# First stage of a decoder trunk: raw input blocks transposed as they land, the norm's factors applied to the weights and to the results

## The chip, the core and the metric

The kernel runs on one core of a Trainium2 chip. The core has five engines, each with an instruction queue of its own: TensorE (PE; its weight loads are listed as PEld), VectorE (DVE), ScalarE (ACT), GpSimd (POOL) and SyncE (SP, which here issues most of the transfers). PE reads from the on-chip buffer and writes its sums into eight accumulator banks (PSUM); ACT and DVE read those banks, POOL does not in this kernel. The engines wait for each other and for transfers by semaphores. The metric is the device time of one execution in microseconds (us).

## What is computed

The reference is a trunk of two layers over 512 positions of 1024 channels. The part that matters here is the beginning of the first layer: a norm of the input, and a projection of it to queries, keys and values of three head groups.

```python
def rms_norm(x, g):
    x32 = x.astype(jnp.float32)
    y = x32 * lax.rsqrt(jnp.mean(x32 * x32, axis=-1, keepdims=True) + EPS)
    return (y * g.astype(jnp.float32)).astype(x.dtype)

def dilated_mixer(xn, w_qkv, w_o, cos, sin):
    qkv = xn @ w_qkv                       # (512, 1024) @ (1024, 2304)
    q, k, v = jnp.split(qkv, 3, axis=-1)
    q = apply_rope(q.reshape(B, T, A_HEADS, HEAD_DIM), cos, sin)
    k = apply_rope(k.reshape(B, T, A_HEADS, HEAD_DIM), cos, sin)
    ...                                    # three groups: banded attention with dilation 1, 4, 16
    return o.reshape(B, T, A_WIDTH) @ w_o

# in reference(), layer 0:
    mix = dilated_mixer(rms_norm(h, g[0]), w_qkv_a[l], w_o_a[l], cos, sin)
```

Behind it follow the attention, a gated feed-forward layer with a short convolution, a shared key/value projection, a second attention and a second feed-forward layer. None of that is changed.

The norm of a row is the row times one number (the reciprocal root of its mean square) times one weight per channel. So `rms_norm(x, g) @ W` equals `diag(r) @ (x @ (diag(g) @ W))`, with `r` one number per position.

## The kernel before

**Precision.** All products are made from halves. A number is split into a high part, rounded to the product's format by a copy, and a low part, the difference; `mm3` (L263) then issues three products: high by high, high by low, low by high (L264, L265, L266). Activations are split when they leave the accumulators, weights by the class `Weights`.

**Weights.** `Weights` (L35) holds a list of pieces of 512 KB, in the order of their use: four pieces for queries and keys of group 0 (pieces 0 to 3, two 128-row chunks each), two for values of group 0 (4 and 5, four chunks each), four for queries and keys of group 1 (6 to 9), four of group 2 (10 to 13), four for values of groups 1 and 2 (14 to 17), then the output projection and the rest of the trunk. `load` issues a piece's transfers on SP (L49), `high` makes the high half on ACT (L57), `low` the low half on DVE (L69). `split(n)` does this up to piece n, `get` hands out the next piece and keeps `ahead` pieces split in advance. Each call of `high` also issues the loads of two pieces more.

**Order.** There is no planner: every engine runs its instructions in the order of the program's text. So the order of the calls at the first stage's end (L1252 to L1289) is the order of work on each engine. SP's transfers are in one queue; the built program gives them eight counters in turn, and a transfer waits until the eighth one before it has landed.

**First stage.** The 512 positions are four blocks of 128. x arrives block by block (`load_x`), interleaved with the weight pieces. The norm's weights arrive as one row, are split in halves on DVE (L246, L247) and spread over all 128 partitions by four products with a row of ones into two PSUM banks (`gain0`, L252). Around these stand warm-up products on zeros (`warm_up`, L231). Then, for each block b:

- the mean square on ACT, the root on ACT, the reciprocal on DVE (`rstd_h`, L268; for block 0 `rstd_shared`, L280, in which ACT and DVE take half of the columns each);
- the norm on DVE, twice 512 columns, times the reciprocal root and times `gain0` (`normed`, L298);
- eight transposes of 128 by 128 on PE into two banks, high halves on ACT (L355), low halves on DVE (L356): `transpose_in` (L342) fills `xT`;
- `qk0`: for each of eight chunks of channels three products of 512 columns into the block's bank, queries and keys of group 0 side by side;
- `qk_post`: ACT copies the bank (L1071), POOL applies the rotary tables (L1077 to L1080).

POOL's `reorder` (L1060) then copies `xT` into `xP`, with positions sorted by their remainder by 4, which groups 1 and 2 use. After the last block, `v_proj0` makes the values of group 0 (L1209; products of 256 columns, `v_ps`), `wide_proj` queries and keys of groups 1 and 2 (`qk_ps` from `xP`) and the values of both, and in between stand the transposes of queries and keys, the scores, the softmax and the probabilities' transposes. DVE also adds rows of the feed-forward weights (`down_sums`) in this time; their transfers go through SP too.

Small tiles come from pools in rotation: `t4` tiles (ten of 4 KB per partition) hold raw weight pieces, x after the norm, rows, values; `t8` tiles (sixteen of 8 KB) hold split pieces and `xT`, `xP`; `bank` hands out the eight PSUM banks in turn.

Of the kernel before, what the change touches and what calls it, by code (L numbers as in the profile page):

```python
# [34 lines left out]
class Weights:  # L35
# [3 lines left out]
    def __init__(self, nc, new_raw, new_pair, pieces):  # L39
        self.nc, self.new_raw, self.new_pair, self.pieces = nc, new_raw, new_pair, pieces  # L40
        self.ahead, self.ahead_dma = 4, 2
        self.raw, self.ready, self.half_done = {}, {}, []
        self.n_dma = self.n_split = self.n_get = 0
# [9 lines left out]
    def high(self, minus=False):  # L53
        if self.n_split < len(self.pieces):
            self.load(self.n_split + 1 + self.ahead_dma)
            raw, pair = self.raw.pop(self.n_split), self.new_pair()
            self.nc.scalar.copy(pair[:, 0], raw)  # L57
            self.half_done.append((raw, pair))
            if minus:
                self.minus()  # L60
# [5 lines left out]
    def low(self):  # L66
        if self.half_done:
            raw, pair = self.half_done.pop()
            self.nc.vector.tensor_tensor(pair[:, 1], raw, pair[:, 0].bitcast(F32), ALU.subtract)  # L69
            self.ready[self.n_split] = (pair[:, 0], pair[:, 1])  # L70
            self.n_split += 1
# [32 lines left out]
def trunk_kernel(ctx, tc, x, norm_gains, w_qkv_a, w_o_a, w_q_b, w_o_b, kv_norm, w_kvf, b_f,  # L104
# [14 lines left out]
    def t4(shape, dt=F32, name="t4"):  # L119
        return p4.tile(shape, dt, tag="t4", name=name)  # L120
# [99 lines left out]
    g_row = t4([1, D], name="g_row")  # L220
    sp.dma_start(g_row, norm_gains[0:1, 0, :])
    ones = sml.tile([1, 128], F32R, tag="ones", name="ones", bufs=1)
    dve.memset(ones.bitcast(F32), 1.0)
# [8 lines left out]
    load_x(0)  # L232
    W.load(3)
    load_x(1)
    W.load(4)
    load_x(2)
# [8 lines left out]
    gr = t4([1, D], F32R, name="gain_h"), t4([1, D], F32R, name="gain_l")  # L245
    dve.tensor_copy(gr[0], g_row)  # L246
    dve.tensor_tensor(gr[1], g_row, gr[0].bitcast(F32), ALU.subtract)  # L247
    gain0 = [bank([128, 512], name="gain00") for _ in range(2)]
    warm_up(4)
    for part in range(2):  # L250
        for i in range(2):
            pe.matmul(gain0[i], ones, gr[part][:, i * 512:(i + 1) * 512], start=part == 0, stop=part == 1)  # L252
    warm_up(4)
# [14 lines left out]
    def rstd_h(b, between=None):  # L268
# [8 lines left out]
        dve.reciprocal(r, sd)  # L277
        return r

    def rstd_shared(b):  # L280

        ss, s2 = small(1, "s1"), small(1, "vr")
        junk, junk2 = (t2([128, 512], BF16, name="junk") for _ in range(2))
        act.activation(junk, h[:, b, 0:512], AF.Square, scale=1.0 / 32, accum_out=ss)
        dve.scalar_tensor_tensor(junk2, h[:, b, 512:1024], 1.0 / 1024, h[:, b, 512:1024], ALU.mult, ALU.mult,
                                 accum_out=s2)
        dve.tensor_scalar(s2, s2, EPS, None, ALU.add)
        sd, r = small(1, "sd"), small(1, "rs")
        act.activation(sd, ss, AF.Sqrt, bias=s2)
        dve.reciprocal(r, sd)  # L290
        return r
# [756 lines left out]
    xn = {}  # L1048
# [18 lines left out]
    def qk_post(g, b, o):  # L1067
# [3 lines left out]
        act.copy(qk.rearrange("p a d -> p (a d)"), o)  # L1071
# [137 lines left out]
    def v_proj0(between):  # L1209
        banks = []  # L1210
        ws = [[t.rearrange("p (k c) -> p k c", k=4) for t in W.get()] for _ in range(2)]
        for b in range(4):
# [9 lines left out]
            if b % 2:  # L1222
                act.copy(V[0][:, b - 1:b + 1, :], banks[b // 2])
                for f in between[b // 2]:
                    f()
# [8 lines left out]
    def norm0(b):  # L1234
        xn[b] = normed(b, rstd_h(b), gain0)

    def transpose0(b, between=None):
        transpose_in(b, xn.pop(b), xT, between)

    def qk0(b, *pieces):  # L1240
        if b not in qk_banks:
            qk_banks[b] = bank([128, T], name="qk_ps")
        for s in pieces:
# [3 lines left out]
            for k in range(2):  # L1247
                kc = 2 * s + k
                ah, al = ax(0, b, kc)
                mm3(qk_banks[b], ah, al, wh[:, k, :], wl[:, k, :], kc == 0, kc == KD - 1)  # L1250
# [12 lines left out]
    transpose0(1)  # L1263
    qk0(0, 3)
    norm0(2)
    qk_post(0, 0, qk_banks[0])
    qk0(1, 0, 1, 2)
    transpose0(2)
# [5 lines left out]
    norm0(3)  # L1274
    qk0(1, 3)
    qk_post(0, 1, qk_banks[1])
    reorder(0, 1)
    qk0(2, 0, 1)
    transpose0(3)
    qk0(2, 2, 3)  # L1280
    W.split(5)
    qk_post(0, 2, qk_banks[2])
    qk0(3, 0, 1, 2, 3)
# [24 lines left out]
    def v_post(g, b, o):  # L1308
# [3 lines left out]
        act.copy(V[1][:, b, :], o[:, 0:256])  # L1312
        dve.tensor_copy(V[2][:, b, :], o[:, 256:512])
# [452 lines left out]
```

## Time and profile before

| | us |
|---|---|
| three runs | 1113.72, 1113.82, 1114.44 (median 1113.82) |
| profiled execution, first to last instruction (span) | 1111.3 |
| PE busy | 1101.0 (99%) |
| DVE busy | 888.2 (80%) |
| ACT busy | 671.9 (60%) |
| POOL busy | 216.7 (20%) |
| first product of the first stage (`qk_ps`) | 9.06 |
| first product of the values (`v_ps`) | 35.02 |

The profiled execution is listed by its span alone; its whole time is not given apart from the three runs. A span runs from the first instruction to the last; what a run takes beside it, start and end, lies outside the profile. Products on PE overlap, and their ends are modelled: a PE that is 99% busy is one that is seldom idle, not one at its peak. Times in the views count from the start of the span. "Idle before" is the time an engine stood still ahead of an instruction, with what released it. The chain of waits is followed back from the last instruction: at each step to what released it, or to the instruction before it on its engine.

### The profile page before, as it was taken

The page shows a single profiled execution, that of the slowest core. Times are in us where ns is not written, and L with a number is a line of the kernel's source. Part 1 is how long each engine was busy: PE and PEld are TensorE (multiplying, and loading weights), DVE is VectorE, ACT ScalarE, POOL GpSimd, SP SyncE. Part 2 cuts the span into 40 slices and gives each one's busy share as a digit, 9 for nine tenths or more (in the row PEclk, how much of TensorE's full clock was granted, in tenths as well). Part 3 has the DMA queues.
Part 4 walks back from the last instruction along what each step waited for, and adds up shares of the span by engine and source line. Part 5 has one row for each costly group of instructions (what it writes and reads, how often), then busy time and mean ns, then how long its engine had stood idle before and what let it go on. Part 6 is the DMA issues. An engine that isn't in the chain of part 4 may idle for free.

```text
span 1111.3 us, 18057 instructions
## 1 busy us (share of the span) xinstructions
PE 1101.0 (99%) x6546; PEld 958.5 (86%) x6546; DVE 888.2 (80%) x1500; ACT 671.9 (60%) x1104; POOL 216.7 (20%) x315
## 2 busy tenths in 40 slices
PE   9999999999999999999999999999999999999997
PEld 6988889899999988888878888889999999988886
DVE  6587788888788689997698777868887788779994
ACT  5454565656666747576462588756656666747572
POOL 2832001311111211000001545500411111211000
PEclk9999999999999999999999999999999999999999
DMA  9499864477887979793447667594378878988862
GB/s 326 171 343 412 319 181 135 87 182 188 212 193 185 247 259 324 280 328 107 133 152 263 212 158 173 187 284 120 83 178 208 195 186 189 241 261 312 318 246 76
DMA packets 185523, 240.46 MB, mean 216 GB/s; under 512 B 11929, under 2 KB 131721, under 8 KB 185434
## 3 DMA queue, kind: packets, MB, share of 16 engines
q1 hardware_dynamic: 170330, 186.61, 51.4%
q0 software_dynamic: 15104, 52.70, 20.8%
q8 instruction: 51, 0.84, 0.3%
q14 instruction: 38, 0.31, 0.1%
HBM read 166.08 MB, written 39.63 MB: 185 GB/s over the span
## 4 chain that ended last, share of the span: by engine, by line
PE 93%; issue 2%; DVE 2%; POOL 1%; DMA 1%; ACT 0%; DVEq 0%; SPq 0%; POOLq 0%
PE up L264 13%; PE up L266 13%; PE up L265 13%; PE acc L264 8%; PE acc L266 8%; PE acc L265 8%; PE qk_ps L264 2%; PE qk_ps L265 2%; PE qk_ps L266 2%; PE v_ps L264 2%; PE v_ps L266 2%; PE v_ps L265 2%; PE first L264 1%; PE first L266 1%; PE first L265 1%
## 5 line engine op out<-in xcount | busy, mean ns | idle before, releaser
L264 PE MATMUL acc<-w 128*128 128x512 f32 (+1 forms) x311 | 120.6, 388 | 0.3 <-DVE mix L326 0.3
L266 PE MATMUL acc<-w 128*128 128x512 f32 (+1 forms) x311 | 120.4, 387 | 0.0
L69 DVE TENSOR_TENSOR w<-wraw,w 128x1024 fp32r<-128x1024 f32 x74 | 97.5, 1333 | 26.0 <-ACT w L57 25.5
L57 ACT CAST w<-wraw 128x1024 fp32r<-128x1024 f32 x94 | 96.7, 1049 | 23.9 <-DMA wraw<-in_w_up_dram 7.4
L265 PE MATMUL acc<-w 128*128 128x512 f32 (+1 forms) x267 | 103.2, 387 | 0.0
L266 PE MATMUL up<-xsh,w 128*128 128x256 f32 x352 | 99.7, 283 | 0.0
L264 PE MATMUL up<-xsh,w 128*128 128x256 f32 x352 | 99.6, 283 | 0.0
L265 PE MATMUL up<-xsl,w 128*128 128x256 f32 x352 | 99.6, 283 | 0.0
L614 ACT ACTIVATE bb<-up,conv 128x512 f32<-128x512 f32 x80 | 59.6, 776 | 58.7 <-DVE up L1001 47.9
L265 PE MATMUL up<-xcl,w 128*128 128x512 f32 (+1 forms) x276 | 93.5, 339 | 0.0
L265 PE MATMUL up<-xbl,w 128*128 128x512 f32 (+1 forms) x276 | 93.5, 339 | 0.0
L264 PE MATMUL up<-xch,w 128*128 128x512 f32 (+1 forms) x276 | 93.5, 339 | 0.0
L264 PE MATMUL up<-xbh,w 128*128 128x512 f32 (+1 forms) x276 | 93.5, 339 | 0.0
L266 PE MATMUL up<-xbh,w 128*128 128x512 f32 (+1 forms) x276 | 93.4, 338 | 0.0
L266 PE MATMUL up<-xch,w 128*128 128x512 f32 (+1 forms) x276 | 93.4, 338 | 0.0
L264 PEld LDWEIGHTS acc<-w 128*128 128x128 f32 x311 | 58.4, 188 | 12.4 <-DVE mix L326 0.7
L266 PEld LDWEIGHTS acc<-w 128*128 128x128 f32 x311 | 58.4, 188 | 11.9
L266 PEld LDWEIGHTS up<-xsh,w 128*128 128x128 f32 x352 | 67.6, 192 | 0.2 <-DMA w<-wsum 0.2
L265 PEld LDWEIGHTS up<-xsl,w 128*128 128x128 f32 x352 | 67.6, 192 | 0.0
L264 PEld LDWEIGHTS up<-xsh,w 128*128 128x128 f32 x352 | 67.6, 192 | 0.0
L615 DVE SCALAR_TENSOR_TENSOR bb<-up,conv,bb 128x511 f32<-128x511 f32 x80 | 59.5, 744 | 6.8 <-ACT bb L614 6.8
L617 DVE SCALAR_TENSOR_TENSOR bb<-up,conv,bb 128x510 f32<-128x510 f32 x80 | 59.9, 749 | 2.8
(315 smaller groups left out, 3152.6 us busy)
## 6 DMA issues: line engine op xcount, KB each, us to landing
wraw<-in_w_up_dram SPq DMA_DIRECT2D x88, 512.0 KB, 5.6
w<-wraw POOLq DMA_DIRECT2D x32, 512.0 KB, 6.6
dT<-dsums SPq DMA_DIRECT2D x28, 512.0 KB, 7.5
w<-wsum POOLq DMA_DIRECT2D x24, 512.0 KB, 5.6
dsums<-in_w_down_dram SPq DMA_DIRECT2D x22, 512.0 KB, 7.8
dsums<-in_w_down_dram SPq DMA_DIRECT2D x44, 256.0 KB, 6.8
hD<-hc POOLq DMA_DIRECT2D x44, 256.0 KB, 7.2
dact<-hD SPq DMA_DIRECT2D x44, 256.0 KB, 5.5
```

The source lines that it names most:

```text
L57: self.nc.scalar.copy(pair[:, 0], raw)
L69: self.nc.vector.tensor_tensor(pair[:, 1], raw, pair[:, 0].bitcast(F32), ALU.subtract)
L264: pe.matmul(o, ah, bh, start=first, stop=False, skip_group_check=shared)
L265: pe.matmul(o, ah, bl, start=False, stop=False, skip_group_check=shared)
L266: pe.matmul(o, al, bh, start=False, stop=last, skip_group_check=shared)
L614: act.activation(bb[:, s, :], ps, AF.Identity, bias=cp[:, 3, ch:ch + 1], scale=cp[:, 2, ch:ch + 1])
L615: dve.scalar_tensor_tensor(bb[:, s, 1:], ps[:, :T - 1], cp[:, 1, ch:ch + 1], bb[:, s, 1:], ALU.mult, ALU.add)
L617: dve.scalar_tensor_tensor(bb[:, s, 2:], ps[:, :T - 2], cp[:, 0, ch:ch + 1], bb[:, s, 2:], ALU.mult, ALU.add)
```

## The change

The norm is taken apart. The raw block is transposed; the channel weights go into the split of the weights; the reciprocal root goes into the evictions.

- `g_row` becomes eight rows of 128, transposed by one product into eight columns (`gcol0`). The two halves of the gain, the row of ones and the four products are gone. Warm-up products: three ahead of the gain's transpose, five behind it, two behind block 0's transposes.
- `Weights.scales` names for pieces 0 to 17 the gain columns of their chunks. For these pieces `high` is an ACT activation with that column as scale, and `low` a DVE operation (raw times column, less the high half), one for each chunk: two of 512 columns a piece, or four of 256 for pieces 4 and 5.
- The transfers of a query/key piece are cut by chunk instead of by query and key. Still two of 256 KB.
- The order of the first loads is x0, pieces 0 and 1, x1, piece 2, x2, piece 3, rotary tables, x3, instead of x0, pieces 0 to 2, x1, piece 3, x2, tables, x3.
- Blocks are transposed straight from `h`. `rstd_shared` and `normed` are not used here any more. `rstd0` makes the mean square, the root and the reciprocal of a block at a later place; the four reciprocals are collected in `rt`.
- `factors_out` writes the four reciprocals of each partition to DRAM and reads them back in the order of `xP` (remainder by 4). Both transfers are on SP. In SP's order they stand behind pieces 4 and 5 and ahead of piece 6 and all that follows.
- The evictions of `qk_post`, `v_proj0` and `v_post` multiply by the reciprocal: activations with a scale on ACT, one tensor-scalar on DVE. `v_proj0` evicts four times 256 columns instead of twice 512.
- The order of the first stage: block 0's chunks 0 to 3, block 1's chunks 0 to 3, then chunks 4 and 5 of both, chunks 6 and 7 of both, then blocks 2 and 3 whole. Blocks 2 and 3 are transposed within that. Pieces 2 and 3 are split later.

```diff
-            self.nc.scalar.copy(pair[:, 0], raw)
+            scales = self.scales.get(self.n_split)
+            if scales is None:
+                self.nc.scalar.copy(pair[:, 0], raw)
+            else:
+                for i, g in enumerate(scales):
+                    s = slice(i * 1024 // len(scales), (i + 1) * 1024 // len(scales))
+                    self.nc.scalar.activation(pair[:, 0, s], raw[:, s], AF.Identity, scale=g)
...
+                    self.nc.vector.scalar_tensor_tensor(pair[:, 1, s], raw[:, s], g, pair[:, 0, s].bitcast(F32),
+                                                        ALU.mult, ALU.subtract)
...
-                v = raw.rearrange("p (k c) -> p k c", k=2)
-                return [(v[:, :, 0:256], cols(wqkv, 2 * s, 2, g * 256, 256)),
-                        (v[:, :, 256:512], cols(wqkv, 2 * s, 2, 768 + g * 256, 256))]
+                v = raw.rearrange("p (k t c) -> p k t c", k=2, t=2)
+                src = wqkv.rearrange("(k p) (t c) -> p k t c", p=128, c=256)
+                return [(v[:, k], src[:, 2 * s + k, g:g + 4:3, :]) for k in range(2)]
...
-    g_row = t4([1, D], name="g_row")
-    sp.dma_start(g_row, norm_gains[0:1, 0, :])
+    g_row = sml.tile([8, 128], F32, tag="grow", name="g_row", bufs=1)
+    sp.dma_start(g_row, norm_gains[0, 0].rearrange("(k p) -> k p", p=128))
...
     load_x(0)
+    W.load(2)
+    load_x(1)
     W.load(3)
-    load_x(1)
+    load_x(2)
     W.load(4)
-    load_x(2)
...
+    warm_up(3)
+    pg0 = bank([128, 8], name="g_ps")
+    pe.transpose(pg0, g_row, ident[:8, :8])
+    gcol0 = sml.tile([128, 8], F32, tag="gcol0", name="gcol0", bufs=1)
+    dve.tensor_copy(gcol0, pg0)
+    warm_up(5)
...
+    for s in range(4):
+        for n in (s, 6 + s, 10 + s, 14 + s):
+            W.scales[n] = columns(2 * s, 2 * s + 1)
+    for s in range(2):
+        W.scales[4 + s] = columns(*range(4 * s, 4 * s + 4))
...
+    def rstd0(b):
+        ss, sd = small(1, "s1"), small(1, "sd")
+        junk = t2([128, D], BF16, name="junk")
+        act.activation(junk, h[:, b, :], AF.Square, scale=1.0 / 32, accum_out=ss)
+        act.activation(sd, ss, AF.Sqrt, bias=eps_t)
+        dve.reciprocal(rt[:, 0, b:b + 1], sd)
+
+    def factors_out():
+        sp.dma_start(rd.rearrange("(b p) -> p b", p=128), rt[:, 0])
+        sp.dma_start(rt[:, 1], rd.rearrange("(l r) -> l r", r=4))
...
-        act.copy(qk.rearrange("p a d -> p (a d)"), o)
+        act.activation(qk.rearrange("p a d -> p (a d)"), o, AF.Identity, scale=factor(g, b))
...
-    xn[0] = normed(0, rstd_shared(0), gain0)
-    W.split(1)
-    transpose0(0, L(W.split, 2))
-    qk0(0, 0)
+    pts = transposed0(0)
+    warm_up(2)
+    high0(0, pts, 0)
+    low0(0, pts, 0)
     W.high()
-    r1 = rstd_h(1, W.low)
-    qk0(0, 1)
+    W.low()
+    high0(0, pts, 1)
+    qk0(0, 0, 1)
     W.high()
-    xn[1] = normed(1, r1, gain0)
     W.low()
+    low0(0, pts, 1)
     qk0(0, 2)
-    transpose0(1)
+    pts = transposed0(1)
+    for i in range(2):
+        high0(1, pts, i)
+        low0(1, pts, i)
     qk0(0, 3)
-    norm0(2)
+    rstd0(0)
+    W.split(3)
+    qk0(1, 0, 1, 2, 3)
+    split0(2)
+    rstd0(1)
+    qk0(0, 4, 5)
+    W.split(4)
+    qk0(1, 4, 5)
+    split0(3)
+    qk0(0, 6, 7)
     qk_post(0, 0, qk_banks[0])
...
+    qk0(1, 6, 7)
     qk_post(0, 1, qk_banks[1])
     reorder(0, 1)
...
+    rstd0(2)
+    rstd0(3)
+    factors_out()
+    qk0(2, *range(4))
     W.split(5)
+    qk0(2, *range(4, 8))
     qk_post(0, 2, qk_banks[2])
-    qk0(3, 0, 1, 2, 3)
+    qk0(3, *range(8))
```

In the changed kernel `qk0` counts chunks, not pieces; `split0(b)` is the block's eight transposes followed by its high and low halves; `high0` is an ACT copy and `low0` a DVE subtraction, as in `transpose_in`; `factor(g, b)` is the column of `rt` for the block, in natural order for group 0 and in `xP`'s order for groups 1 and 2.

More of the change, by code (lines that the diff above doesn't have):

```diff
@@ L41, in __init__ @@
         self.ahead, self.ahead_dma = 4, 2
+        self.scales = {}
         self.raw, self.ready, self.half_done = {}, {}, []
@@ L243, in trunk_kernel, with columns @@
     make_identity(nc, ident)
[L245 to L253, printed above, removed]
+    warm_up(3)
[4 more added lines that the diff above has]
+    warm_up(5)
+    def columns(*ks):
+        return [gcol0[:, k:k + 1] for k in ks]
+    for s in range(4):
[3 more added lines that the diff above has]
+        W.scales[4 + s] = columns(*range(4 * s, 4 * s + 4))
     mask0 = cst.tile([128, 256], F32, name="mask0")
@@ L276, in rstd_h @@
         r = small(1, "rs")
[L277 to L289, printed above, removed]
         dve.reciprocal(r, sd)
@@ L1222, in v_proj0 @@
             if b % 2:
-                act.copy(V[0][:, b - 1:b + 1, :], banks[b // 2])
+                for i in range(2):
+                    act.activation(V[0][:, b - 1 + i, :], banks[b // 2][:, i], AF.Identity, scale=factor(0, b - 1 + i))
                 for f in between[b // 2]:
@@ L1232, in trunk_kernel, with transposed0, high0, low0 @@
     ws, qk_banks = {}, {}
[L1234 to L1240, printed above, removed]
+    def transposed0(b):
+        pts = []
+        for i in range(2):
+            pt = bank([128, 4, 128], name="xt_ps")
+            for k in range(4):
+                pe.transpose(pt[:, k, :], h[:, b, (4 * i + k) * 128:(4 * i + k + 1) * 128], ident)
+            pts.append(pt)
+        return pts
+    def high0(b, pts, i):
+        act.copy(xT[0][i][:, :, b * 128:b * 128 + 128], pts[i])
+    def low0(b, pts, i):
+        s = slice(b * 128, b * 128 + 128)
+        dve.tensor_tensor(xT[1][i][:, :, s], pts[i], xT[0][i][:, :, s].bitcast(F32), ALU.subtract)
+    def qk0(b, *kcs):
         if b not in qk_banks:
             qk_banks[b] = bank([128, T], name="qk_ps")
-        for s in pieces:
+        for kc in kcs:
+            s, k = kc // 2, kc % 2
             if s not in ws:
@@ L1311, in v_post @@
                 V[i] = t4([128, 4, 256], name=f"V{i}")
-        act.copy(V[1][:, b, :], o[:, 0:256])
-        dve.tensor_copy(V[2][:, b, :], o[:, 256:512])
+        act.activation(V[1][:, b, :], o[:, 0:256], AF.Identity, scale=factor(1, b))
+        dve.tensor_scalar(V[2][:, b, :], o[:, 256:512], factor(2, b), None, ALU.mult)
     down0 = down_sums([*[(0, j) for j in range(ND)], (1, 8)], in_one, sp, 1, 1)
```

33 lines of the change are left out of this document (18 added, 15 removed).

## The prediction

> **What bounds the kernel now.** I read the page first (the span, then the chain's shares by engine).
>
> ```profile
> span 1111.3 us, 18057 instructions
> ...
> PE 93%; issue 2%; DVE 2%; POOL 1%; DMA 1%; ACT 0%; DVEq 0%; SPq 0%; POOLq 0%
> ```
>
> TensorE (PE) carries 93% of the chain that ended last. So a change of the first stage is worth exactly what it moves the moment from which PE runs without waiting, unless it makes a later wait. The chain of waits for the first 60 us, in order of time (start, length, what), shows where that moment lies:
>
> ```profile
> 5.42 1.82 PE warm L231 x4
> 7.30 1.10 PE xt_ps L348 x4
> ...
> 11.13 0.69 DVE xal L356
> 11.81 1.02 DVE w L69
> ...
> 13.72 0.74 DVE xn L298
> 14.46 1.15 DVE w L69
> 15.65 0.50 PE qk_ps L265
> ...
> 21.15 0.87 PE xt_ps L348 x8
> ```
>
> Up to 15.65 us the chain is VectorE (DVE) with a little ScalarE (ACT): norm products (L298), low halves of x (L356) and of the weights (L69). From 15.65 us it is PE. Four transposes take 1.10 us at 7.30 and eight take 0.87 us at 21.15: PE still ran at half rate there. Next the PE timeline, where the first stage's products (`qk_ps`) begin and end and the values' products (`v_ps`) begin:
>
> ```profile
> 9.06 0.80 PE L264 MATMUL qk_ps<-w,xah 128*128 128x512 f32 x1
> ...
> 20.99 1.03 PE L348 MATMUL xt_ps<-ident,xn 128*128 128x128 f32 x8
> 21.78 0.47 PE L264 MATMUL qk_ps<-w,xah 128*128 128x512 f32 x1
> ...
> 33.66 0.39 PE L264 MATMUL qk_ps<-w,xah 128*128 128x512 f32 x1
> ...
> 34.80 0.39 PE L266 MATMUL qk_ps<-w,xal 128*128 128x512 f32 x1
> 35.02 0.28 PE L264 MATMUL v_ps<-w,xah 128*128 128x256 f32 x1
> ```
>
> A product of 512 columns costs (34.80-33.66)/5 = 0.228 us, a block of eight transposes 21.78-20.99 = 0.79 us. Four blocks x 8 chunks x 3 = 96 products and three later blocks of transposes need 96x0.228+3x0.79 = 24.3 us. From 9.06 to 35.02 are 26.0 us, so 1.7 us are waits. The stage has two losses: a first product at 9.06 us, and 1.7 us behind it. All else on PE stays.
>
> **The change, part by part.** The rows with its prices, grouped by form (count | busy, mean ns):
>
> ```profile
> L614 ACT ACTIVATE bb<-up,conv 128x512 f32<-128x512 f32 x80 | 59.6, 776 | 58.7 <-DVE up L1001 47.9 <-PE up L266 10.8
> ...
> L721 ACT CAST w<-wraw 128x512 fp32r<-128x512 f32 x22 | 13.6, 620 | 0.0
> ...
> L1071 ACT COPY qk<-qk_ps 128x512 f32<-128x512 f32 x12 | 6.7, 589 | 10.2 <-PE qk_ps L266 7.3 <-DMA dT<-dsums 3.0
> ...
> L506 ACT ACTIVATE xqh<-nT,gcol 128x512 fp32r<-128x512 f32 x8 | 5.4, 716 | 0.1
> ...
> L69 DVE TENSOR_TENSOR w<-wearly,w 128x1024 fp32r<-128x1024 f32 x6 | 7.9, 1315 | 1.4 <-ACT w L57 1.3
> ...
> L507 DVE SCALAR_TENSOR_TENSOR xql<-nT,gcol,xqh 128x512 fp32r<-128x512 f32 x8 | 5.7, 748 | 0.1
> ```
>
> L506 and L507 are the very forms that the new split uses. A weight piece in two scaled halves costs ACT 2x0.716 = 1.43 us instead of 1.05 (the row at 6.78, below) and DVE 2x0.748 = 1.50 instead of 1.32. Neighbours of an engine overlap by about 0.1 us, as the two-in-a-row rows show:
>
> ```profile
> 21.62 1.07 ACT L355 CAST xah<-xt_ps 128x512 fp32r<-128x512 f32 x2 [3.78 <-PE xt_ps L348]
> ...
> 550.87 1.34 ACT L506 ACTIVATE xqh<-nT,gcol 128x512 fp32r<-128x512 f32 x2
> ...
> 552.30 1.41 DVE L507 SCALAR_TENSOR_TENSOR xql<-nT,gcol,xqh 128x512 fp32r<-128x512 f32 x2
> ```
>
> So I space ACT's scaled halves by 0.62 us, its copies out of PSUM by 0.48 and DVE's halves by 0.66. Against the dearer split stand eight norm products (L298; 0.74 us in the chain's row), gone from DVE, and a gain row that is one transpose instead of two DVE passes and four products.
>
> Now the new start. x0 and the first weight piece (W0) keep their places in SP's queue:
>
> ```profile
> 0.74 0.36 SPq L221 DMA_DIRECT2D g_row<-in_norm_gains_dram  x1
> ...
> 2.22 0.68 DVE L246 CAST gain_h<-g_row 1x1024 fp32r<-1x1024 f32 x1 [0.92 <-DMA g_row<-in_norm_gains_dram]
> ...
> 4.80 0.63 ACT L284 ACTIVATE junk<-h 128x512 bf16<-128x512 f32 x1 [2.57 <-DMA h<-in_x_dram]
> ...
> 6.78 1.05 ACT L57 CAST w<-wearly 128x1024 fp32r<-128x1024 f32 x1 [0.70 <-DMA wearly<-in_w_qkv_a_dram]
> ...
> 8.25 0.33 SPq L211 DMA_DIRECT2D h<-in_x_dram  x1
> ...
> 9.02 1.12 SPq L49 DMA_DIRECT2D wearly<-in_w_qkv_a_dram  x2
> ```
>
> x0 has landed at 4.80. PE stands ready about then: three warm-up products, the gain's transpose (its row lands at 2.22), five more, at (1.82/4) 0.45 us each from 1.2 us: 4.95. Four transposes at half rate take 1.10, so ACT starts the first high half of x at 6.05 instead of 8.42. ACT goes on: x high 6.05, W0a 6.53, W0b 7.15 (landed by 6.78), x high 7.77, W1a 8.25, W1b 8.87. (SP uses eight counters in turn; a load waits for the eighth before it. So the load at 8.25 says that W1 had landed, the one at 9.02 that W2a had.) DVE: x low 6.66, W0a low 7.28 to 8.03, W0b low to 8.69, W1a low 9.0 to 9.75, W1b low to 10.4, x low to 11.0.
>
> PE: eight transposes to 6.75, two warm-ups, **first product at 7.6**. Its partner needs W0a low (8.06), and the second of chunk 2 needs W1a low (9.78 where pure pace gives 9.2: 0.58 lost). Block 1's transposes stand at 10.2; x1 takes W2's place among the loads (9.0 to 9.6), so they do not wait. Block 1's first low-half product waits 0.26 for DVE (12.42), chunk 6 of block 0 waits 0.2 for W3a low, since ACT has a whole-row square ahead of it (twice the 0.63 of the half row at 4.80). Lost: 1.04 us. Values begin at 7.6+24.3+1.0 = 32.9 instead of 35.02: **2.1 us**. With an early clock it is up to 2.8, with a late one 1.0 to 1.7 (the rivals below).
>
> Squares, roots and reciprocals leave the path: they are needed at the evictions (20.9 us on). The cover is 5 to 15 us of products.
>
> Evictions with a scale from PSUM are not in the trace. The copy (589) is the lower bound, L614 with scale and bias (776) the upper; L506 less L721 (96 ns) says 0.69 us. 16 evictions add 0.1 each, covered by PE; at 776 they still are. W4 and W5 go in four parts of 256 columns: each between 0.26 (a quarter of 1.05) and 0.716 on ACT; I take 0.46, halfway, some 1.9 us a piece. They begin at 26 and end by 30, against a need at 32.9. Even at 0.716 (ends by 32) PE does not wait.
>
> SP: two small transfers (the reciprocals out and back) stand ahead of W6 and all later loads. Their issue waits for the last reciprocal, at 26 us. Today those loads go out here:
>
> ```profile
> 11.03 3.84 SPq L49 DMA_DIRECT2D wraw<-in_w_qkv_a_dram  x4
> ...
> 18.53 4.60 SPq L49 DMA_DIRECT2D wraw<-in_w_qkv_a_dram  x6
> ...
> 41.41 1.29 DVE L1089 COPY qkT<-qkT_ps 128x512 f32<-128x512 f32 x2 [0.71 <-PE qkT_ps L1086]
> ...
> 48.43 1.61 PE s_ps L1111 x16
> 50.04 0.43 PE qk_ps L264
> ...
> DMA to landing us min/median/max: 5.4/6.3/8.7
> ```
>
> The nearest row for a small transfer through an idle queue is g_row: issued 0.74, landed 2.22, 1.5 us; with 512 packets of four bytes I take 2.5, and 1.5 back: 4 us. The upper bound is twice the 6.3 us median of the weight pieces (the last row, of L49's view): 12.6. W6 then goes out at 30.5, and W8, 2.6 MB later at 0.34 MB/us (256 KB between 8.25 and 9.02, above) plus some 2.5 us, lands at 40.5; its low half is done at 41.9. Behind it in ACT's and DVE's order stand the values' evictions and the qkT copies (1.3 us), which PE's scores need at 48.4-2.0 = 46.4. Margin 3.2 us: cost nothing.
>
> POOL: its reorder must end its first half before PE's next stage.
>
> ```profile
> 26.13 1.11 POOL L1060 CAST xph<-xah 128x512 fp32r<-128x512 f32 x1
> ...
> 29.32 2.12 POOL L1060 CAST xpl<-xal 128x512 fp32r<-128x512 f32 x1
> ...
> 45.69 1.14 POOL L1060 CAST xpl<-xal 128x512 fp32r<-128x512 f32 x1
> ```
>
> Today it ends at 46.8 for a start at 50.04. The reorder would begin at 24.8 (block 1's eviction at 22.3 to 23.0, the rope behind it), 1.3 us earlier than at 26.13, but POOL loses about 0.75 us per us of DVE work on weights (2.12 instead of 1.1 beside an L69): 46.3 against 47.9. Margin 1.6.
>
> The Trainium skill (TensorE: Matmul & The Clock Gate, "PE-mode transpose") says that transposes do not count as busy for the clock; the table of states there asks for about 3.4 us of sustained work. Here PE was busy from 1.35 us, yet its transposes at 7.30 were at half rate. By the rule the warm-ups alone (1.2 to 5) release the clock or nothing does before the products; the sum would be 2.7 by the first, 1.0 by the second.
>
> **The rivals.** (a) The forecast, 1.6 to 2.3 us gained. (b) *The early clock*: warm-ups without the four gain products between them (one row of inputs) release PE by 5 us; four transposes take 0.8 instead of 1.1, all behind shifts by 0.3 and the waits of 0.26 and 0.2 close: 2.3 to 2.8 gained, 1111.2. For it: a denser start. Against: seven busy microseconds did not do it before. (c) *The late clock*: half rate until about 9.6 as today makes the nine first products cost 0.43; the waits hide most, 0.3 lost, 1112.1; until 11.5, 1.1 lost, 1112.9. (d) *A new wait at about 46 us*, the other side: the round trip holds the loads on SP. It costs PE nothing up to 7.2 us of trip, eats the gain at 9.2, and makes the kernel slower by 2.2 us at 11.4. At the upper bound of 12.6: 5.4 of waiting, 3.4 slower, 1117.2. For it: every later load is behind it, and 512 packets of four bytes are in no row. Against: g_row's 1.5 us. (e) *The reorder is late*: POOL losing all of DVE's 7 us of weight work instead of 0.75 of it ends at 48.1 and costs 0.2 to 1: 1112.5. (f) It changes nothing: only if PE were bound before 15.65 by something kept; the chain names removed work (L298, L69's order), so little.
>
> **How the numbers follow.** The profiled span is 1111.3 us; the runs' median of 1113.82 lies 2.5 above it, which I carry unchanged. 1111.3-2.0+2.5 = **1111.8 us** (2.1 less 0.1 for small new waits). A measurement can tell 0.2% (2.2 us) from no change, so the forecast lies just inside that. Chances: (a) 0.47, of it 0.12 above 2.2; (b) 0.26; (c) 0.09; (d) 0.11, nearly all of it past 11.4 us of trip; (e) 0.05; (f) 0.02. Faster by over 0.2%: 0.12+0.26 = 0.38. Slower: 0.10, from (d). Same: 0.52. Range 1110.5 ((b) with 0.7 more) to 1114.2 ((c), (e), (f), and (d) up to a trip of 9.6); what is left out is (d)'s rest and a tenth for what I have not seen.
>
> **What would show it.** First `qk_ps` product at 7.6 (7.2 to 8.1), first `v_ps` product at 32.9 (32.3 to 33.6), PE idle in 12 to 33 us below 0.6. Transposes of block 0 straight after x0. ACT's split halves at 0.71. W6's load out near 30 us with no wait of PE in 33 to 50; a PE wait there on `xph`, `qkT` or a weight would mean (d) or (e). Wrong if the values begin early but the gain is gone by 140 us.

## The result and the profile after

The changed kernel took 1118.44 us (median of 9 runs, 1117.51 to 1121.08), the kernel before 1114.44 us (9 runs, the three above among them, 1113.72 to 1117.24). The ratio is 1.0038, with a 95% interval of 1.0029 to 1.0047: slower by 4.2 us (3.2 to 5.2). The profiled execution took 1118.3 us, of which the span is 1116.5; the span before was 1111.3.

First the page of the changed kernel: the span, and the shares of the chain that ended last.

```profile
span 1116.5 us, 18086 instructions
PE 85%; DMA 6%; DVE 4%; issue 3%; ACT 1%; POOL 1%; DVEq 0%; SPq 0%; POOLq 0%; ACTq 0%
```

PE's share fell from 93% to 85%, and transfers (DMA) rose from 1% to 6%. These shares say which way the chain went, not how much was lost: 8% of the span would be some 90 us. PE's timeline tells where the loss is (start, duration, line, operation, count, and in brackets the idle time with what ended it):

```profile
7.15 0.50 PE L283 MATMUL qk_ps<-w,xah 128*128 128x512 f32 x1 [0.43 <-ACT w L64]
...
32.76 0.28 PE L283 MATMUL v_ps<-w,xah 128*128 128x256 f32 x1
...
45.13 1.04 PE L1107 MATMUL qkT_ps<-ident,qk 128*128 128x128 f32 x8
49.80 3.10 PE L1132 MATMUL s_ps<-qkT 64*128 64x128 f32 x16 [3.62 <-DVE qkT L1110]
52.82 0.65 PE L283 MATMUL qk_ps<-w,xph 128*128 128x512 f32 x1
```

The first stage did what it was forecast to do: the first product at 7.15 (before 9.06), the values from 32.76 (before 35.02), 2.26 us gained. Then PE stood 3.62 us ahead of the scores (`s_ps`), and the sixteen score products took 3.10 us where they had taken 1.61. The first product of the next stage (from `xph`) began at 52.82; before, this row had 49.97. So 2.26 us ahead had become 2.85 behind within 20 us. The chain of waits names the cause (start, length, what):

```profile
25.73 9.14 DMA rd<-rt
34.88 4.15 DMA rt<-rd
39.05 7.64 DMA wraw<-in_w_qkv_a_dram
46.78 0.73 ACT w L64
47.57 0.83 issue
48.40 0.74 DVE w L82
49.14 0.61 DVE qkT L1110
49.80 3.10 PE s_ps L1132 x16
```

The reciprocals' write to DRAM (`rd<-rt`) took 9.14 us, the read back 4.15; then piece 8 was loaded, split on ACT and DVE, and only behind that, in DVE's order, stood the copies of `qkT` for which the scores wait. SP's own timeline shows what was held:

```profile
9.68 1.11 SPq L50 DMA_DIRECT2D wearly<-in_w_qkv_a_dram  x2
25.73 0.37 SPq L1065 DMA_DIRECT2D rd<-rt  x1
34.88 0.34 SPq L1066 DMA_DIRECT2D rt<-rd  x1
35.27 1.96 SPq L50 DMA_DIRECT2D wraw<-in_w_qkv_a_dram  x4
...
39.05 4.87 SPq L50 DMA_DIRECT2D wraw<-in_w_qkv_a_dram  x6
```

SP issued nothing from 10.8 to 25.73 (it waited for the last reciprocal) and nothing to 34.88 (it waited for the write to land). Pieces 6 and 7 then went out at once. Piece 8 is the eighth transfer behind the read back, so by the counters in turn it waited until that had landed, at 39.03. Before, pieces 6 to 10 went out from 11.03 on.

Behind 53 us the same PE instruction started 3.0 to 3.3 us later than before, up to 970 us. Another 1.9 us went at 980, where a product waited for an added weight half:

```profile
980.23 0.39 PE L285 MATMUL up<-xsh,w 128*128 128x256 f32 x1 [1.68 <-DMA w<-wsum]
```

That makes the 5.2 us between the two spans. The runs below show that the second part comes and goes between executions, and that the first stays in every version of the changed kernel that leaves the long write ahead of pieces 6 to 8 or beside them.

### The profile page after: what moved, and what is told of

Its sections match the earlier page's. It is cut to its first block, busy times and chain, and to the rows that moved or that the text cites. A ratio compares the mean times of both kernels' runs of the same rounds, so it can differ in the third digit from the quotient of the medians.

```text
span 1116.5 us, 18086 instructions
## 1 busy us (share of the span) xinstructions
PE 1100.3 (99%) x6545; PEld 958.5 (86%) x6545; DVE 894.2 (80%) x1509; ACT 680.4 (61%) x1128; POOL 214.7 (19%) x315
## 4 chain that ended last, share of the span: by engine, by line
PE 85%; DMA 6%; DVE 4%; issue 3%; ACT 1%; POOL 1%; DVEq 0%; SPq 0%; POOLq 0%; ACTq 0%
PE up L285 12%; PE up L283 12%; PE up L284 12%; PE acc L283 8%; PE acc L285 8%; PE acc L284 8%; DMA w<-wsum 2%; PE qk_ps L283 2%; PE qk_ps L284 2%; PE qk_ps L285 2%; PE o_ps L1692 2%; PE s_ps L1644 1%; PE first L285 1%; PE first L283 1%; PE first L284 1%
## 5 line engine op out<-in xcount | busy, mean ns | idle before, releaser
L78 DVE TENSOR_TENSOR w<-wraw,w 128x1024 fp32r<-128x1024 f32 x62 | 82.2, 1346 | 21.6 <-ACT w L60 21.0
L60 ACT CAST w<-wraw 128x1024 fp32r<-128x1024 f32 x82 | 84.3, 1048 | 19.8 <-DMA dsums<-in_w_down_dram 6.9
```

## The experiments

Three theories stood at the start. T: the loss is SP's hold of pieces 6 to 10 by the trip (the write of the reciprocals to DRAM and the read back). R1: the dearer weight split is what is late; DVE's halves of pieces 6 and 7 took 6.18 us for four (L82, at 40.79) beside POOL instead of four times 0.75. R2: most of the loss lies behind 53 us.

A table for all of them first. It gives the start of a PE instruction less the start of the same instruction in the profiled execution before (us), at four places, and the times.

| kernel | first `xph` products | 705 us | 722 us | end | median, us | ratio to before (95%) |
|---|---|---|---|---|---|---|
| the change | 3.0 | 3.2 | 3.3 | 5.3 | 1118.4 | 1.0038 (1.0029 to 1.0047) |
| e1_loads_first | -2.1 | -2.4 | -1.8 | -1.2 | 1111.7 | 0.9982 (0.9972 to 0.9991) |
| e2_before_trip | 0.3 | 0.4 | 1.0 | 1.1 | 1114.2 | 0.9999 (0.9990 to 1.0008) |
| e3_rows_out | -2.3 | -2.7 | -0.6 | 0.3 | 1112.8 | 0.9984 (0.9974 to 0.9994) |
| e4_back_later | 3.9 | 3.9 | 6.0 | 7.7 | 1119.1 | 1.0030 (1.0019 to 1.0042) |
| e5_out_on_act | 0.5 | 1.3 | 2.1 | 3.6 | 1116.8 | 1.0023 (1.0010 to 1.0035) |
| e6_fill_wait | 1.7 | 2.0 | 2.0 | 2.4 | 1116.4 | 1.0019 (1.0008 to 1.0030) |
| e7_both | -1.8 | -2.1 | -1.6 | -1.5 | 1113.9 | 0.9990 (0.9978 to 1.0001) |
| e8_row_out_gather_back | -2.1 | -2.3 | -1.7 | -1.3 | 1111.2 (one run) | |
| e9_row_out_timed (e8 again) | -2.1 | -1.5 | 0.6 | 1.5 | 1113.3 | 0.9969 (0.9956 to 0.9983) |
| e10_spaced | -2.5 | -2.3 | -0.2 | 1.5 | 1114.5 (one run) | |
| e11_fill_less | 2.5 | 2.9 | 3.4 | 3.8 | 1116.9 (one run) | |
| e12_before_longer | 14.4 | 14.4 | 14.6 | 14.6 | 1127.4 (one run) | |

The first column is the effect of the edits. What is added behind it (at 705 to 722 and at 970 to 980 us) differs between e8 and e9, which are the same kernel, by 2.8 us. Ratios compare with runs of the kernel before on the same chip, whose medians were 1114.0 (e1 to e4), 1114.7 (e5 to e8) and 1115.4 (e9 to e12).

### e1: the loads ahead of the trip

```diff
     rstd0(3)
+    W.load(11)
     factors_out()
```

> Pieces 6 to 10 go out on SP ahead of the two small transfers; nothing else changes. Theory T (SP's queue: the hold until the last reciprocal at 25.7 us and the 13.3 us of the round trip make pieces 6 to 10 late): no wait of ACT for a piece, scores (`s_ps`) at 46.2 instead of 49.80 (the 48.43 of before less the 2.26 gained by 33 us), at full rate (1.6 us for the sixteen), the first `qk_ps` product from `xph` at 47.8 (before 50.04, with the change 52.89); time 1114.4-2.2 = 1112.2, 1111 to 1113. Rival R1 (the dearer split is what is late: VectorE's halves on pieces 6 to 8 took 1.55 us each beside POOL instead of 0.75): the halves still take six times 1.55 behind piece 5's end at 35.05, so the qkT copies start at 44.4 or later and end at 46.9, scores at 46.5 to 48.4, time 1113 to 1114.4. Rival R2 (most of the loss comes after 53 us): group 1 begins at 47.8, yet the time is 1116 or more.

SP's timeline of e1, then PE's:

```profile
11.45 9.37 SPq L50 DMA_DIRECT2D wraw<-in_w_qkv_a_dram  x10
25.86 0.37 SPq L1065 DMA_DIRECT2D rd<-rt  x1
35.59 0.34 SPq L1066 DMA_DIRECT2D rt<-rd  x1
```

```profile
46.23 1.68 PE L1132 MATMUL s_ps<-qkT 64*128 64x128 f32 x16
47.84 0.50 PE L283 MATMUL qk_ps<-w,xph 128*128 128x512 f32 x1
```

The trip is as long as ever (9.73 us from the write's issue to the read's), and yet the scores begin at 46.2 without a wait, at full rate, and the next stage at 47.84. T's numbers were met, time included; R1 and R2 fall. One line moved makes the change a gain of 2.0 us (1.0 to 3.1).

### e2 and e12: the trip in the kernel before

```diff
     reorder(0, 1)
+    sp.dma_start(rd.rearrange("(b p) -> p b", p=128), rt[:, 0])
+    sp.dma_start(rt[:, 1], rd.rearrange("(l r) -> l r", r=4))
```

The lines left out collect the four reciprocals in the tile `rt`.

> The kernel before, with the four reciprocals of the first norm collected in one tile, written to DRAM and read back on SP at the place the change has them, ahead of piece 6; what is read back is not used. Theory T: the loss without any other part of the change. The trip starts at the last reciprocal (24.5), piece 6 goes out at 34, piece 8 at 37.8, landing at 45.4, its split ends near 48, the qkT copies near 50.5; the first `qk_ps` product from `xph` at 52.1 to 53.6 instead of 50.04; time 1116.5 to 1118. R1 (dearer splits): 50.0 and 1114.4, no change.

T was wrong here: the time did not move, though the hold was there (piece 6 out at 33.86 instead of 11.03). DVE's and PE's timelines of e2 show how close it was:

```profile
46.05 1.32 DVE L69 TENSOR_TENSOR w<-wraw,w 128x1024 fp32r<-128x1024 f32 x1 [1.83 <-ACT w L57]
47.29 2.47 DVE L1092 COPY qkT<-qkT_ps 128x512 f32<-128x512 f32 x4
```

```profile
48.66 1.68 PE L1114 MATMUL s_ps<-qkT 64*128 64x128 f32 x16
```

The copies began at 47.29 and PE was free for the scores at 48.66. The scores can start some 0.74 us behind the copies' start (49.06 and 49.80 in the changed kernel), so 0.6 us of room was left. In the changed kernel the copies began at 49.06, 1.77 later (the last reciprocal 0.9 later, the write 0.5 longer, the split dearer), and PE was free at 46.18, 2.5 earlier: 1.8+2.5-0.6 = 3.7, about the wait of 3.62. So the hold alone costs nothing; it is the hold together with a first stage that wants the same data 2.5 us sooner. e12 writes twice, to see whether the kernel before stands at the edge:

> e2_before_trip with the write done twice, one after the other, so that pieces 6 to 10 of the kernel before are held 8.6 us longer. In e2 the copies of qkT ended just as the scores could start (PE waited 0.2 us), so the kernel before had that much room and no more. If so, every microsecond beyond it counts: scores at 57 instead of 48.7, at half rate behind so long a wait, first product from `xph` at 59.5 to 60.5 instead of 50.3, time 1122.5 to 1124.5. If the kernel before does not depend on these pieces there, 50.3 and 1114.

```profile
60.39 3.10 PE L1114 MATMUL s_ps<-qkT 64*128 64x128 f32 x16 [11.78 <-DVE qkT L1092]
```

It does, within that room, and the loss is larger than expected. Piece 6 went out at 43.52, 9.7 later than in e2 (the second write took 9.7, not 8.6); piece 8 was issued at 50.0, 12.4 later than in e2, since the issue of the four transfers ahead of it took 4.95 us instead of 1.96. Scores at 60.4, at half rate, and the next stage 13 to 14 us late.

### e3, e8, e9 and e10: what the write's price is made of

e3 transposes the reciprocals on PE and writes four rows of 512 bytes:

```diff
-        sp.dma_start(rd.rearrange("(b p) -> p b", p=128), rt[:, 0])
+        pe.transpose(tp, rt[:, 0], ident)
+        dve.tensor_copy(g_row[0:4, :], tp)
+        sp.dma_start(rd.rearrange("(b p) -> b p", p=128), g_row[0:4, :])
```

The bank for the transpose (`tp`) is left out here. The edit also moves the trip in the program's text from ahead of block 2's products to behind six of its chunks, and the split of piece 5 from behind four to behind six; the write was issued 0.7 us later (26.39 instead of 25.73).

> The changed kernel with the reciprocals transposed on PE and written as four rows of 512 bytes instead of 512 packets of four bytes; the way back and the place in SP's queue stay. If the packets make the price (T1): the write lands within 2.5 us instead of 9.1, piece 8 goes out at about 33.6 instead of 39.05 and lands at 41.2, no wait of PE at the scores, first product from `xph` at 47.8 to 48.2, time 1112.2 to 1112.8. If any write to DRAM followed by a read takes that long (T2): again 9 us, loads one microsecond later than with the change (the transpose and the copy), time 1118 to 1119.5.

SP's timeline of e3: the read's issue follows the write's landing, 1.2 us after the write's issue instead of 9.1.

```profile
26.39 0.28 SPq L1068 DMA_DIRECT2D rd<-g_row  x1
27.57 0.34 SPq L1069 DMA_DIRECT2D rt<-rd  x1
27.96 1.97 SPq L50 DMA_DIRECT2D wraw<-in_w_qkv_a_dram  x4
```

No wait was left at the scores (46.06), the next stage began at 47.68: T1, the packets make the price. Even with pieces 6 to 10 behind the last reciprocal and behind the trip there is time enough, if the trip is short. e8 keeps PE out of it and turns the layout: 128 packets of 16 bytes out, 512 elements gathered back.

```diff
-        sp.dma_start(rd.rearrange("(b p) -> p b", p=128), rt[:, 0])
-        sp.dma_start(rt[:, 1], rd.rearrange("(l r) -> l r", r=4))
+        sp.dma_start(rd.rearrange("(p b) -> p b", b=4), rt[:, 0])
+        for b in range(4):
+            sp.dma_start(rt[b * 32:b * 32 + 32, 1], rd.rearrange("(j r b) -> b j r", r=4, b=4)[b])
```

> The changed kernel with the layout in DRAM turned: the write goes out as 128 packets of 16 bytes, and the read back gathers 512 elements of four bytes, in four transfers. If the number of small packets written is the price (9.14 us for 512, 0.28 for each of the 32 that one of 16 engines has): the write takes 8x0.28 = 2.3 to 3.5 us, pieces 6 and 7 go out at 29 to 30.5; if reading four bytes costs what writing them does, the pieces behind the read crawl until about 39 and the loss stays; if only writes do, piece 8 goes out by 36 and the first product from `xph` is at 48 to 50.

```profile
25.86 0.34 SPq L1065 DMA_DIRECT2D rd<-rt  x1
27.29 2.60 SPq L1067 DMA_DIRECT2D rt<-rd  x4
```

The write landed within 1.43 us, less than the 2.3 to 3.5 that a price per packet gave. Each of the four reads landed after 2.0 us, pieces 6 and 7 went out at 29.93, and the next stage began at 47.85, without a wait of PE: here reading four bytes apiece was cheap, writing them side by side was not. e9 timed this kernel:

> e8_row_out_gather_back again, timed: 128 packets of 16 bytes out, 512 elements gathered back, at the change's own place ahead of piece 6. Its profile had the first product from `xph` at 47.85 against 52.9 with the change and 50.04 before, and one time of 1111.2. If the 512 four-byte packets were all of the loss, the median is 1111.3 to 1112.3, as e1_loads_first (0.998 of the kernel before); if the short trip still costs something, above 1112.5.

1113.28 us against 1115.41 for the kernel before on that chip: ratio 0.9969. The absolute band was missed because all kernels were slower there; the gain of 3.5 us (1.9 to 4.9) is, as far as the intervals tell, no smaller than e1's. e10 leaves the 512 four-byte packets and moves them 64 bytes apart (`rd` as 512 rows of 16 numbers, of which the first is used):

> The changed kernel with the 512 four-byte packets written 64 bytes apart instead of side by side; the read gathers them from there. If each small packet costs 0.28 us on its engine whatever lies beside it, the write lands after 9 us again and the first product from `xph` is at 52 to 53.5. If the price is packets that fall into the same stretch of DRAM and wait for one another (the rows of 16 bytes in e8, 128 packets, took 1.4 us in all), it lands within 3 us and the product begins at 47.9 to 48.5.

```profile
25.44 0.37 SPq L1065 DMA_DIRECT2D rd<-rt  x1
27.28 0.64 SPq L1066 DMA_DIRECT2D rt<-rd  x1
```

1.84 us instead of 8.5 to 10.0 in the kernels that pack them, and the next stage at 47.43. The same number of packets of the same size: so it is their lying side by side in DRAM that costs 7 to 8 us, not their number alone. The 128 packets of 16 bytes in e8 lie side by side too and cost nothing like it; what packets between 4 and 16 bytes, or another distance than 64, would cost, no run shows.

The changed kernel's trace shows where the time does not go. Its DMA packets from 26.5 to 27.1 us, then from 27.1 to 34.9:

```profile
DMA packets 528, 0.00 MB, mean 4 GB/s; under 512 B 528, under 2 KB 528, under 8 KB 528
DMA packets 0, 0.00 MB, mean 0 GB/s; under 512 B 0, under 2 KB 0, under 8 KB 0
```

By the records, the DMA engines were through with the 512 packets (and 16 more) in 0.6 us. Then no packet moved for 7.8 us, until the write counted as landed. So the price is no price per packet on its engine, as e8's and e10's expectations put it (0.28 us). What the chip waits for behind the packets, no run shows.

### e4 and e5: behind the write, and beside it

e4 leaves the write in place and puts the read back behind the loads:

```diff
     next(sums)
+    W.load(11)
+    factors_back()
     reorder(2, 3)
```

> The changed kernel with the write at its place and the read back behind pieces 6 to 10. SP still stands until the last reciprocal (25.7), but no longer until the write has landed. T: piece 6 goes out at 26.1. Of SP's eight counters in turn the one of the write comes back to piece 8 (the eighth transfer behind it), so piece 8 goes out when the write has landed, at 34.9 instead of 39.05, and lands at 41 to 42: no wait of PE, first product from `xph` at 47.8 to 48.2, time 1112.2 to 1112.8. If the hold until 25.7 matters by itself, the time is above 1114. If no counter is in the way, piece 8 goes out before 30.

The counter was where T had it (piece 8 out at 35.90, when the write had landed), but the time was as bad as the change's. First SP's timeline of e4, then its transfers between 25 and 36 us in 40 slices (GB/s):

```profile
25.91 0.37 SPq L1065 DMA_DIRECT2D rd<-rt  x1
26.32 2.04 SPq L50 DMA_DIRECT2D wraw<-in_w_qkv_a_dram  x4
...
35.90 6.84 SPq L50 DMA_DIRECT2D wraw<-in_w_qkv_a_dram  x6
```

```profile
GB/s 0 0 0 0 0 0 2 5 0 52 48 30 11 0 0 0 0 0 0 19 71 115 63 15 22 22 60 37 15 30 19 7 45 22 37 11 7 30 19 22
```

Pieces 6 and 7 were issued at 26.3 to 28.4 and moved at some 25 GB/s on the mean until the write had landed, where transfers reach 350 to 400 afterwards. So the write does not only make SP wait: it holds what is behind it. Piece 8 then landed at 45.7, with all the rest in front of it. The hold until the last reciprocal does not explain this by itself: e3 and e8 have it too and lost nothing. e5 puts the write on ACT's queue, and a one-packet write in its place on SP:

```diff
-        sp.dma_start(rd.rearrange("(b p) -> p b", p=128), rt[:, 0])
+        sp.dma_start(rd1[:, None].rearrange("b o -> o b"), rt[0:1, 0])
+        act.dma_start(rd.rearrange("(b p) -> p b", p=128), rt[:, 0])
```

> As e4_back_later (read back behind pieces 6 to 10), but the 512-packet write goes out on ScalarE's queue, and SP has in its place a write of one packet of 16 bytes from the same tile, so that its loads are still held until the last reciprocal (25.9) and then run beside the write. In e4 the loads issued from 26.3 on moved 21 GB/s until the write had landed at 35.9. Theory Q (the write holds only the transfers behind it in its own queue): pieces 6 and 7 land before 31, piece 8 goes out before 31, no wait of PE at the scores, first product from `xph` at 47.8 to 48.3, time 1112 to 1113. Theory E (the packets hold the 16 DMA engines themselves, which serve both queues; the Trainium skill, DMA: Bandwidth & Descriptors, "Issuing engines are not separate DMA queues", would have it so): the loads crawl until about 36 all the same, first product from `xph` at 52 to 53.5, time 1116.5 to 1119.

Stretches of e5 (from and to in us, busy time of PE, PEld, DVE, ACT and POOL, PE's clock, share of the DMA engines, GB/s):

```profile
28.00:32.00 4.00, 4.00 (x20) 3.30 (x19) 4.00 (x5) 2.18 (x6) 4.00 (x4) 1.00 0.43 30
32.00:36.00 4.00, 4.00 (x31) 3.81 (x30) 3.47 (x4) 0.69 (x1) 3.92 (x6) 1.00 0.48 22
36.00:40.00 4.00, 4.00 (x37) 4.00 (x36) 1.03 (x1) 1.41 (x2) 3.92 (x8) 1.00 0.74 206
```

22 to 30 GB/s on SP's queue while the write was under way on ACT's: theory Q falls. That DMAs of all issuing engines run on the same 16 DMA engines and interleave, the Trainium skill says (DMA: Bandwidth & Descriptors, "Issuing engines are not separate DMA queues"), and that a second queue did not help agrees with it. But theory E's reason, that the packets hold these engines, is not what the trace shows. ACT's queue in e5 from 26 to 28 us (packets, MB, share of the 16 engines):

```profile
q10 hardware_dynamic: 528, 0.00, 13.1%
```

The write's packets were all through by 28 us, and the loads crawled until 36. Whether the engines, the DRAM or something between them is held, stays open. The time, 1116.77, is in its band. The product at 50.45 is not: piece 8's high half began at 44.66 instead of 46.78, PE waited 2.30 us, and this time its clock did not fall:

```profile
48.69 1.83 PE L1136 MATMUL s_ps<-qkT 64*128 64x128 f32 x16 [2.30 <-DVE qkT L1114]
```

### e6 and e11: the clock behind the wait

e6 puts products whose result nobody reads into PE's wait:

```diff
+    def fill():
+        o = bank([128, T], name="fill_ps")
+        for i in range(14):
+            pe.matmul(o, ax(0, 0, 0)[0], xT[0][0][:, 0, :], start=True, stop=True)
...
-             [..., L(qk_transpose, 0, 3), L(scores, 0, 0), ...
+             [..., L(qk_transpose, 0, 3), fill, L(scores, 0, 0), ...
```

> The changed kernel with fourteen products of 512 columns, whose result nobody reads (3.2 us at 0.228), ahead of the scores on PE, in the 3.6 us in which PE waited there. The hold stays as it is, so the scores still begin at 49.8. Theory C (1.5 of the 5.1 us lost at this place are a clock that fell during the wait, since the sixteen scores took 3.10 us instead of 1.61): they take 1.6 us, the first product from `xph` begins at 51.3 to 51.5 instead of 52.9, time 1118.4-1.5 = 1116.9 (1116.3 to 1117.5). If the slow scores have another cause (their operands come late one by one, or the processor behind them), 52.9 and 1118.4 as before, or more by what the products add.

```profile
46.15 3.44 PE L1252 MATMUL fill_ps<-xah 128*128 128x512 f32 x14
49.99 1.74 PE L1132 MATMUL s_ps<-qkT 64*128 64x128 f32 x16 [0.40 <-DVE qkT L1110]
51.66 0.50 PE L283 MATMUL qk_ps<-w,xph 128*128 128x512 f32 x1
```

The stretch from 50 to 51 us of the changed kernel and of e6, in which the scores run (PE's clock is the third number from the end):

```profile
50.00:51.00 1.00, 1.00 (x10) 1.00 (x12) 1.00 (x3) 0.96 (x1) 0.00 (x0) 0.50 1.05 393
50.00:51.00 1.00, 1.00 (x12) 0.92 (x14) 1.00 (x2) 1.00 (x1) 0.00 (x0) 1.00 1.09 407
```

The added products in the gap bring the scores back to full rate: the granted clock is 1.00 instead of 0.50, and they take 1.67 us from their start to the next product instead of 3.02. The next stage comes 1.2 us earlier (51.66, a little behind the expected 51.3 to 51.5), and the ratio to the kernel before falls from 1.0038 to 1.0019. So of the 5.1 us between 33 and 53 us, 3.6 were the wait and 1.5 the clock: theory C. e11 fills less:

> As e6_fill_wait, with three of the idle products instead of fourteen, so that PE still waits some 2.9 us (3.6 less 0.7). A wait of 2.3 us (e5) left the scores at 1.7 us, waits of 3.4 and 3.6 made them 3.1. If the clock follows the length of the wait with an edge near 3.4 us (the Trainium skill, TensorE: Matmul & The Clock Gate, "Idle/cold", has one window of about 3.4 us), the scores take 1.6 to 1.8 us and the first product from `xph` begins at 51.3 to 51.6; if the edge lies lower, 3.1 us and 52.9.

```profile
45.76 0.93 PE L1252 MATMUL fill_ps<-xah 128*128 128x512 f32 x3
49.42 3.09 PE L1132 MATMUL s_ps<-qkT 64*128 64x128 f32 x16 [2.73 <-DVE qkT L1110]
```

Half rate behind 2.73 us of idling: less than the 3.4 us of the window in the Trainium skill's table (TensorE: Matmul & The Clock Gate, "Idle/cold") is enough. An edge between 2.3 (e5) and 2.73 is not shown by this: it is one execution of each kernel, and waits of one length went both ways elsewhere, as the section on later waits shows.

### e7: both mends together

The edits of e1 and e3 in one kernel.

> e1_loads_first and e3_rows_out together: pieces 6 to 10 ahead of the trip, and the reciprocals written as four rows of 512 bytes. If the hold of pieces 6 to 10 was all the loss, nothing is left for the short trip to win: first product from `xph` at 47.8, time as e1_loads_first, 1111.7 (1111.0 to 1112.3). If the loads of the later sums, which stood behind the long trip until 36.0 and go out at 28 now, matter further on (a later wait at 640 to 720 or 975 us), up to 1 us less.

The next stage began at 48.17, and the ratio, 0.9990 (0.9978 to 1.0001), is no better than e1's. That the loads of the later sums went out 7.5 us earlier (28.47 instead of 35.98) brought PE nothing. The median, 1113.88, lies above the band, on a chip on which the kernel before was 0.7 slower.

### What comes later and differs from run to run

Two later waits of PE make the rest of the table. One is ahead of the transposes of the second attention's probabilities at 711 us (1.58 us in the kernel before). Stretch 712 to 716 us of e1 and of e9, both behind a wait of 2.1 to 2.2 us there (the clock is the third number from the end):

```profile
712.00:716.00 4.00, 4.00 (x27) 3.20 (x28) 3.11 (x12) 2.92 (x10) 2.24 (x3) 1.00 0.51 200
```

```profile
712.00:716.00 4.00, 4.00 (x16) 3.46 (x15) 3.12 (x14) 3.05 (x11) 2.75 (x3) 0.59 0.66 261
```

The same wait left the clock alone in e1 and took it down in e9. Between 705 and 722 us e1 lost 0.6 us against the kernel before and e9 2.1, so the clock cost 1.5. The wait's length does not decide it: of the kernels with 2.08 to 2.16 us there, the clock fell in e3, e4, e9 and e10 and stayed in e1, e2, e7, e8 and e11, and e8 and e9 are the same kernel with the same 2.08 us. The other is the wait for the added weight half at 975 to 980 (0 to 1.9 us). Neither stands in code that the change edits.

## Why the prediction was wrong

- **The step that failed: the round trip on SP, "4 us".** It was taken from `g_row`'s 1.5 us, a read of one row, for a write of 512 four-byte packets. The write took 9.14, the read back 4.15: 13.3, beyond the upper bound of 12.6 too, which was built from whole weight pieces. "Margin 3.2 us: cost nothing" falls with it; piece 8 landed at 46.7, not 40.5.
- **Rival (d) is what happened.** Place, waiting engine and order of events (piece 8, its low half, the copies, the scores) were as written, the chance was 0.11. Its formula gives 13.3-7.2 = 6.1 us of waiting; PE waited 3.6. It let pieces 6 to 8 all follow the whole trip, so that piece 8 would have landed at 40.5+9.3 = 49.8; pieces 6 and 7 went out when the write had landed, 3.8 us ahead of the read's landing, and piece 8 landed at 46.7. What it left out is the clock behind the wait, 1.5 us (e6). The two errors partly cancel: 5.1 lost where the formula has 6.1, 2.85 slower at 53 us where it has 4.1.
- **What a long write does to others was not in the sum.** Even with SP free the loads would have crawled (e4, e5).
- **The first product, "7.6".** 7.15: the chain has the four transposes at 5.13 in 0.73 us, not 1.10. That is nearer to rival (b), which gave them 0.8; its further gain went into waits. The values at 32.76 against "32.9"; 32.76-7.15-24.3 = 1.3 us of waits against 1.04. The 2.1 us are there in e1 (2.13 at the next stage), and 2.0 of them in the time.
- **The split, "0.716 and 0.748".** 715 and 749 ns on pieces 0 to 3. Not seen: DVE's parts of 256 columns took 1206 ns each beside POOL's copies, so that piece 5 ended at 35.05 and not at 30. PE did not wait for it.
- **The evictions, "0.69".** 690 ns. **The reorder:** its first half ended at 41.8, not 46.3; the cover was larger than claimed.
- **The signs.** "A PE wait there on `xph`, `qkT` or a weight would mean (d) or (e)" read the result rightly: `qkT`. Piece 6's load, expected near 30 us, went out at 35.27.

Forecast and median differ by 6.6 us: 5.1 were lost ahead of 53 us, and 0.6 is the kernel before, whose median is 1114.44 over nine runs and was 1113.82 over the first three. The 0.9 left by subtraction is no more than what the later waits added in single executions (2.3 in the profiled one); no run splits it further.

## What to carry to other kernels

A transfer that waits for a late result belongs behind the loads that wait for nothing: on an in-order queue it delays all of them by its own wait, here 15 us, before it has cost anything. Write small results to DRAM as rows, or apart from each other, never as neighbouring four-byte packets, and price such a transfer by a row of its own kind or by a wide range. When a stage becomes earlier, look at what its successor needs at the new time: the same hold cost nothing before and 5 us after.

## What the runs showed of the hardware

- A write of 512 four-byte packets side by side in DRAM took 8.5 to 10.0 us; the same packets 64 bytes apart 1.84, 128 packets of 16 bytes 1.43, four of 512 bytes 1.18 (each from the write's issue to the read's). The Trainium skill (DMA: Bandwidth & Descriptors, Specifications) has every write below 512 bytes read, modify and write; by these runs being below 512 bytes costs 0.7 us at most by itself (1.84 against 1.18), and the rest came only with four-byte neighbours. Its packets were through within 0.6 us in the changed kernel, 7.8 us before it had landed. While the write was under way, other loads moved at some 20 to 30 GB/s instead of 350 to 400, on its own queue (e4) and on another (e5).
- PE's clock was at half rate behind idle times of 3.62 (change), 3.43 (e4) and 2.73 us (e11), and not behind 2.30 (e5); at 711 us, waits of 2.08 to 2.16 us took it down in four kernels and not in five. The Trainium skill (TensorE: Matmul & The Clock Gate, the table of states) gives one idle window of about 3.4 us and calls the window free-running. That equal waits go either way agrees with the second; that 2.73 and 2.08 us were enough does not agree with the first.
